# Sparse attention in a two-block transformer kernel: split products of probabilities and values replaced by plain float32 ones, and the scaling of the probabilities moved into the transposing product

## The chip, the cores and the metric

The kernel runs on one core of one Trainium2 chip. The metric is the device time of one execution in microseconds. A core has a matrix engine (TensorE, PE in the profile, with its weight loads as PEld), a vector engine (VectorE, DVE), a scalar engine (ScalarE, ACT), GpSimd (POOL) and SyncE (SP). Each works through its own instructions in order, and semaphores join them. Transfers are issued from SP's and POOL's queues.

## The reference, cut to what matters

The program is two transformer blocks on 512 tokens of width 1024. The part that the change touches is the sparse attention (`nsa_mixer`) of the second block: 16 heads of width 64 in 4 groups, which share keys and values within a group. Each head attends in three branches, to compressed keys, to selected blocks and to a window, and the branches are summed with gates:

```python
p_c = masked_softmax(s_c, (cmp_end[None, :] <= t[:, None])[None, None, :, None, :])
o_c = jnp.einsum('bgqhn,bngd->bqghd', p_c.astype(v_cmp.dtype), v_cmp)
...
p_s = masked_softmax(s_s, (dist_s >= 0)[:, :, :, None, :])
o_s = jnp.einsum('bgqhk,bgqkd->bqghd', p_s.astype(v_g.dtype), v_g)
...
p_w = masked_softmax(s_w, m_w[None, None, :, None, :])
o_w = jnp.einsum('bgqhk,bkgd->bqghd', p_w.astype(vw_b.dtype), vw_b)
out = gb[..., 0:1] * o_c + gb[..., 1:2] * o_s + gb[..., 2:3] * o_w
```

Everything is float32. At 512 tokens the selected blocks and the window take in every earlier token, so that these two branches are causal attention over 512 keys, with different keys and values and the same relative bias.

## The kernel before

A matrix product of two float32 matrices is written as products of float32r halves nearly everywhere: a number is split into a high part (a copy cast to float32r on ACT) and a low part (the difference, a subtraction on DVE), and the products of the parts are summed in PSUM. `split` (L157) and `wsplit` (L212) do this, and `gemm_g` (L229) issues three products for each pair of 128x128 weights and 128x512 activations (L243 to L245).

The sparse attention runs in the phase `pa2` (L1475). Three streams are woven into one program order there by `weave` (L57), with the weights written beside them: `nsa` (the attention), `rwkv_backs` followed by `merge` (the recurrence of the other mixer, then the branch products), and `merge_gates` (a plain matrix product). The framework's scheduler makes each engine's order from this.

`nsa` goes through 4 groups, `nsa_group` (L1166) through the group's 4 heads. `nsa_pre` (L1112) prepares a group: the stacked queries, the split keys of the first of the two branches, and the compressed branch's probabilities, transposed and split into `pc`. Each head calls `attend` twice (L1192, `br` 1 and 2) with a gate, 32 calls in all. The pooling block in front calls it eight times without a gate.

`attend` (L299) works on 512 queries by 512 keys under the causal mask, in four tiles of queries of 128, 256, 384 and 512 keys. For each tile it makes the scores (L311, L312), adds the bias and takes the minimum on DVE (L313), and takes the exponential on ACT with the row's sum (L315). Then come the reciprocals and the gate (L316, L318), and each tile is scaled by them, two on ACT (L321) and two on DVE (L323). Ten blocks of 128x128 are transposed (L328) into PSUM, in four strips of 512, 384, 256 and 128 columns. Each strip is split (L330 on ACT, L331 on DVE), and two products (L332, L333) add it to the head's output `o`. Their stationary operand is V with its high part in 64 columns and its low part in the other 64, so `o` has the two parts' sums in its two halves. The compressed branch adds its share in the same way (L1188). `o_evac` (L335) sums the halves with a copy on ACT (L340) and an addition on DVE (L341).

`nsa_values` (L1155) loads a pair of groups' values and splits them (L1161 to L1164). Transfers of this stage that `self.side` issues are on POOL's queue: queries, keys, values and each head's bias tile (L1183).

Of the kernel before, what the change touches and what calls it, by code (L numbers as in the profile page):

```python
# [8 lines left out]
F32 = mybir.dt.float32  # L9
F32R = mybir.dt.float32r  # L10
I32 = mybir.dt.int32
AF = mybir.ActivationFunctionType
OP = mybir.AluOpType
# [25 lines left out]
class Gen:  # L39
# [259 lines left out]
    def attend(self, qst, kst, bias, V, o, first, last, gate=None):  # L299

        nc = self.nc
        kh, kl = kst
        st = self.f("sm", shape=(128, 32))
        m, s, r = st[:, 0:4], st[:, 4:8], st[:, 8:12]
        Pt = self.f("p", shape=(128, 1280))
        P = [Pt[:, 64 * i * (i + 1):64 * (i + 1) * (i + 2)] for i in range(4)]
        for i, pt in enumerate(P):
            w = 128 * (i + 1)
            ps = self.ps("a")
            qt = qst[:, i * 128:i * 128 + 128]  # L310
            nc.tensor.matmul(ps[:, :w], qt, kh[:, :w], start=True, stop=False)  # L311
            nc.tensor.matmul(ps[:, :w], qt, kl[:, :w], start=False, stop=True)  # L312
            nc.vector.tensor_tensor_reduce(pt, ps[:, :w], bias[:, 512 - w:], 1.0, 3e38, OP.add, OP.min,  # L313
                                           m[:, i:i + 1])
            nc.scalar.activation(pt, pt, AF.Exp, bias=m[:, i:i + 1], scale=-1.0, accum_out=s[:, i:i + 1])  # L315
        nc.vector.reciprocal(r, s)  # L316
        if gate is not None:
            nc.vector.tensor_tensor(r, r, gate, OP.mult)  # L318
        for i, pt in enumerate(P):
            if i >= 2:  # L320
                nc.scalar.activation(pt, pt, AF.Copy, scale=r[:, i:i + 1])  # L321
            else:
                nc.vector.tensor_scalar(pt, pt, r[:, i:i + 1], None, op0=OP.mult)  # L323
        for j in range(4):
            w = 512 - 128 * j
            ps = self.ps("b")
            for i in range(j, 4):
                nc.tensor.transpose(ps[:, (i - j) * 128:(i - j + 1) * 128], P[i][:, j * 128:j * 128 + 128], self.ident)  # L328
            ph, pl = self.f("pt", F32R), self.f("pt", F32R)
            nc.scalar.copy(ph[:, :w], ps[:, :w])  # L330
            nc.vector.tensor_tensor(pl[:, :w], ps[:, :w], ph[:, :w].bitcast(F32), OP.subtract)  # L331
            nc.tensor.matmul(o[:, j * 128:], V(j), ph[:, :w], start=first and j == 0, stop=False)  # L332
            nc.tensor.matmul(o[:, j * 128:], V(j), pl[:, :w], start=False, stop=last and j == 3)  # L333
# [724 lines left out]
    def nsa_compressed(self):  # L1058
        nc, A, V, S = self.nc, self.A, self.nc.vector, self.nc.scalar
        k = lambda n, w: self.rp.tile([128, w], F32R, name=n, tag=n, bufs=1)  # L1060
        self.cmp = kc2, vc = (k("kch", 128), k("kcl", 128)), k("vc", 512).rearrange("p (g s d) -> p g s d", g=4, s=2)
        self.gt = self.rp.tile([128, 4, 48], F32, name="gt", tag="gt", bufs=1)
        self.nsa_consts()
        yield 3.0
        w2 = self.const("w2kv", [128, 2, 192])
        nc.sync.dma_start(w2, A["c2"].rearrange("k p n -> p k n"))

        def load(i):
            t = self.f("src")
            nc.sync.dma_start(t, self.kvd[i])  # L1070
            return t
        hk = yield from self.compress([load(0), load(1)], "k")
        yield 10.0
        p = self.ps("b")
        for ct in range(2):
            nc.tensor.matmul(p[:, :128], w2[:, ct, 0:128], hk[ct], start=ct == 0, stop=ct == 1)
        kc, sq = self.f("f")[:, :128], self.f("f")[:, :128]
        S.copy(kc, p[:, :128])
        S.activation(sq, kc, AF.Square)
        col = self.norm_col(sq[:64])  # L1080
        p = self.ps("b")
        nc.tensor.transpose(p[:, :128], col[:, 0:1].to_broadcast([128, 128]), self.ident)
        V.scalar_tensor_tensor(kc, kc, self.vec("k_gain", 0), p[:, :128], OP.mult, OP.mult)
        kch, kcl = kc2
        S.copy(kch, kc)
        V.tensor_tensor(kcl, kc, kch.bitcast(F32), OP.subtract)
        hv = yield from self.compress([load(2), load(3)], "v")
        yield 10.0
        p = self.ps("b")[:, :256].rearrange("p (g d) -> p g d", g=4)
        hx = []  # L1090
        for ct in range(2):
            hx.append(self.f("f"))
            S.copy(hx[ct].rearrange("p (g h n) -> p g h n", g=4, h=4),
                   hv[ct].rearrange("p (g n) -> p g n", g=4)[:, :, None].to_broadcast([128, 4, 4, 32]))
        for g in range(4):
            for ct in range(2):
                nc.tensor.matmul(p[:, g], hx[ct][:, 128 * g:128 * g + 128], w2[:, ct, 128:192], start=ct == 0, stop=ct == 1)
        S.copy(vc[:, :, 0], p)
        V.tensor_tensor(vc[:, :, 1], p, vc[:, :, 0].bitcast(F32), OP.subtract)
        yield 1.0  # L1100

    def norm_col(self, sq):
# [9 lines left out]
    def nsa_pre(self, g):  # L1112
# [4 lines left out]
        kst = {1: self.split(k1, tag="kst")}  # L1117
# [30 lines left out]
        ps = self.ps("b")  # L1148
        for i in range(4):
            nc.tensor.transpose(ps[:, i * 128:i * 128 + 128], e[:, i * 128:i * 128 + 128], self.ident)  # L1150
        pc = self.split(ps, tag="pc")
        yield 2.0
        return qst, kst, pc

    def nsa_values(self, gp):  # L1155
        nc, V, S = self.nc, self.nc.vector, self.nc.scalar
        VT = self.VT = self.f("vt", F32R, (128, 4 * 4 * 128)).rearrange("p (t k n) -> p t k n", t=4, k=4)
        for t2 in range(2):
            z = self.f("ld").rearrange("p (t k d) -> p t k d", t=2, d=64)
            for t in range(2):  # L1160
                self.side.dma_start(z[:, t].rearrange("p k d -> p (k d)"), self.vd[gp, 2 * t2 + t])  # L1161
            v = VT[:, 2 * t2:2 * t2 + 2]
            S.copy(v[:, :, :, 0:64], z)
            V.tensor_tensor(v[:, :, :, 64:128], z, v[:, :, :, 0:64].bitcast(F32), OP.subtract)  # L1164

    def nsa_group(self, g, qst, kst, pc):  # L1166

# [7 lines left out]
        for h in range(4):  # L1175
            hd = 4 * g + h
            par = h % 2
            if par == 0:
                O = self.f("o")
            if h == 2 and g < 3:  # L1180
                self.ahead = self.nsa_loads(g + 1)
            bias = self.f("bias")
            self.side.dma_start(bias, bass.AP(tensor=self.grd.tensor, offset=self.grd.offset + hd * 1280 + 127,  # L1183
                                              ap=[[576, 2], [-1, 64], [1, 512]]))
            o = self.ps("o")
            hs = slice(32 * h, 32 * h + 32)
            for i in range(2):
                nc.tensor.matmul(o, vc[hs, g].rearrange("p s d -> p (s d)"), pc[i][hs], start=i == 0, stop=False)  # L1188
            ready = self.nsa_pre(g + 1) if h == 3 and g < 3 else iter(())
            for br in (1, 2):  # L1190
                kv = 2 * (br - 1) + gl
                self.attend(qst[h], kst[br], bias, lambda j: VT[:, j, kv], o,  # L1192
                            False, br == 2, gate=self.gt[:, :, 3 * hd + br])
                yield 3.6
                if br == 1:
                    try:
                        while True:
                            yield next(ready)
                    except StopIteration as done:
                        pre = done.value  # L1200
            self.o_evac(O, o, par)
            if par == 1:
                pr = hd // 2
                nc.sync.dma_start(self.ynd[pr], O)
                if "y_n" in self.dbg:
                    nc.sync.dma_start(self.dbg["y_n"][pr * 128:(pr + 1) * 128], O)
# [30 lines left out]
    def merge(self, live):  # L1237
# [29 lines left out]
            yield w  # L1267
        while "" in live:
            yield None
        load, product_n = self.branch(A["w_br_n"], self.ynd, 8, second, ["kst"] * 3 + ["qst"] * 2 + ["pt"] * 2 + [("p", 1280)],  # L1270
                                      "f", "f")
        yield from self.side_by_side([product, load])
        yield from self.side_by_side([product_n, residual()])
# [169 lines left out]
def emit(tc, A, out, dbg={}):  # L1443
    nc = tc.nc
    with ExitStack() as ctx:
# [14 lines left out]
        with g.phase("rec"):  # L1460
# [11 lines left out]
                g.weave(("", g.rwkv_fronts(xs), 245), ("_p", others(), 170))  # L1472
            g.banks = {"a": "01", "b": "23", "n": "2", "o": "4", "a_b": "5", "b_b": "6", "g_m": "7", "g_b": "56"}
            g.side = nc.gpsimd
            with g.phase("pa2", f=3, ld=3, qst=5, kst=6, p=2, pt=4, bias=2, pc=2, kz=1, o=1, ot=1, vt=1,  # L1475
                         kb=1, v=1, bk=1, ys=1, vs=2, vu=2, yc=6, vgb=2, y=2, f_m=1, **{"as": 1}):
                g.reserve(kb=1024, v=512, vs=1024, vu=1024, yc=128, bk=1024, y=1024, ys=1024,
                          vgb=512, ld=512, kst=512, vt=2048, qst=512, f=512, pc=512, bias=512)

                live = {"", "_m"}  # L1480

# [146 lines left out]
```

## Time and profile before

| what | value |
|---|---|
| median of 3 runs | 2083.45 us (2080.49 to 2084.88) |
| the profiled execution | 2082.19 us, span of its instructions 2080.4 us |
| mean granted TensorE clock over the span | 0.981 |
| PE, PEld busy | 2004.5 us (96%), 1627.0 us (78%) |
| DVE, ACT, POOL busy | 1308.6 us (63%), 925.3 us (44%), 95.5 us (5%) |

Busy time is the union of an engine's records. Records of matmuls are pipelined: one begins before the one ahead of it has ended, so their lengths don't add up to time, and their distances do. L12 is line 12 of the kernel. `x32` counts instructions. "out<-in" names the tiles.

### The profile page before, as it was taken

What the parts mean: (1) busy time and instruction counts of PE and PEld (TensorE: products, weight loads), DVE (VectorE), ACT (ScalarE), POOL (GpSimd) and SP (SyncE); (2) the same over time, 40 slices, a digit from 0 to 9 for tenths busy, and PEclk for the clock granted to TensorE, in tenths of its full rate; (3) what the DMA queues carried; (4) which work ended last, traced back from release to release, by engine and by line L of the source; (5) the groups of instructions that cost most, each with busy time, mean ns of one, the idle gap of its engine ahead of it and who ended that gap; (6) DMA issues with size and microseconds to landing.
All of it is one profiled execution on the core that took longest, in us unless ns stands there. A gap on an engine that the chain in (4) does not pass through costs nothing.

```text
span 2080.4 us, 27852 instructions
## 1 busy us (share of the span) xinstructions
PE 2004.5 (96%) x9927; PEld 1627.0 (78%) x9927; DVE 1308.6 (63%) x3007; ACT 925.3 (44%) x1778; POOL 95.5 (5%) x167
## 2 busy tenths in 40 slices
PE   8999999999999899899988899999999999999999
PEld 7778888888888677777767687887878778888887
DVE  5785432554463568687848988888466756666522
ACT  4874531442254233333346577777243443333311
POOL 0000000000003200000120111000000000000000
PEclk9999999999999999999989899999999999999999
DMA  5222332333355754755673445446442123333332
GB/s 161 82 85 93 99 93 92 117 108 120 117 185 158 171 147 141 183 147 168 191 168 105 129 122 145 126 123 190 154 140 84 41 81 92 101 92 98 95 109 84
DMA packets 178267, 256.75 MB, mean 123 GB/s; under 512 B 95409, under 2 KB 109953, under 8 KB 178129
## 3 DMA queue, kind: packets, MB, share of 16 engines
q1 hardware_dynamic: 162832, 231.31, 38.2%
q0 software_dynamic: 15296, 23.66, 3.9%
q8 instruction: 79, 1.29, 0.3%
q14 instruction: 60, 0.48, 0.1%
HBM read 205.12 MB, written 45.53 MB: 120 GB/s over the span
## 4 chain that ended last, share of the span: by engine, by line
PE 46%; DVE 6%; ACT 3%; issue 2%; DMA 2%; SPq 0%; POOL 0%; DVEq 0%; ACTq 0%; POOLq 0%
PE psg L243 8%; PE psg L245 8%; PE psg L244 8%; PE psg_b L243 1%; PE psg_b L244 1%; PE psg_b L245 1%; PE psb L328 1%; DVE ys L777 1%; PE psg_p L243 1%; PE psg_p L244 1%; PE psg_p L245 1%; PE pso L332 1%; PE psa L744 1%; DVE ys L778 1%; PE pso L333 1%
## 5 line engine op out<-in xcount | busy, mean ns | idle before, releaser
L222 ACT CAST wh<-ws 128x1024 fp32r<-128x1024 f32 (+2 forms) x283 | 291.6, 1031 | 697.9 <-PE psg L244 457.1
L223 DVE TENSOR_TENSOR wl<-ws,wh 128x1024 fp32r<-128x1024 f32 (+2 forms) x283 | 339.4, 1201 | 266.3 <-ACT wh L222 265.7
L243 PE MATMUL psg<-xh,wh 128*128 128x512 f32 x984 | 392.2, 399 | 4.7 <-ACT wh L222 4.7
L245 PE MATMUL psg<-xh,wl 128*128 128x512 f32 x984 | 393.1, 399 | 0.0
L244 PE MATMUL psg<-act,wh 128*128 128x512 f32 x912 | 359.7, 395 | 1.1 <-DVE act L166 1.1
L243 PEld LDWEIGHTS psg<-xh,wh 128*128 128x128 f32 x984 | 186.0, 189 | 46.8 <-ACT wh L222 5.5
L245 PEld LDWEIGHTS psg<-xh,wl 128*128 128x128 f32 x984 | 186.0, 189 | 41.5 <-issue 1.2
L244 PEld LDWEIGHTS psg<-act,wh 128*128 128x128 f32 x912 | 171.1, 188 | 42.8 <-DVE act L166 1.5
L243 PE MATMUL psg<-act,wh 128*128 128x512 f32 x496 | 196.1, 397 | 2.8 <-ACT act L165 1.4
L245 PE MATMUL psg<-act,wl 128*128 128x512 f32 x496 | 196.1, 396 | 0.5 <-DVE wl L223 0.5
L244 PE MATMUL psg<-xl,wh 128*128 128x512 f32 x352 | 139.7, 397 | 0.0
L243 PEld LDWEIGHTS psg<-act,wh 128*128 128x128 f32 x496 | 92.8, 188 | 27.2 <-ACT act L165 2.2
L245 PEld LDWEIGHTS psg<-act,wl 128*128 128x128 f32 x496 | 93.0, 187 | 23.7 <-DVE wl L223 1.3
L315 ACT ACTIVATE p<-p,sm 128x128 f32<-128x128 f32 (+3 forms) x160 | 89.6, 561 | 15.0 <-DVE sm L313 13.6
L331 DVE TENSOR_TENSOR pt<-psb,pt 128x512 fp32r<-128x512 f32 (+3 forms) x160 | 75.8, 487 | 20.0 <-ACT pt L330 17.7
L244 PE MATMUL psg<-x,wh 128*128 128x512 f32 x216 | 88.2, 409 | 0.0
L313 DVE CUSTOM_DVE_ANT_0 p<-psa,bias 128x128 f32<-128x128 f32 (+3 forms) x160 | 75.9, 485 | 8.2 <-PE psa L312 6.1
L328 PE MATMUL psb<-ident,p 128*128 128x128 f32 x400 | 75.3, 285 | 2.5 <-DVE y L921 0.9
L244 PEld LDWEIGHTS psg<-xl,wh 128*128 128x128 f32 x352 | 66.3, 188 | 14.0
L330 ACT CAST pt<-psb 128x512 fp32r<-128x512 f32 (+3 forms) x160 | 65.8, 424 | 25.7 <-PE psb L328 20.8
L243 PE MATMUL psg_p<-xh,wh 128*128 128x512 f32 x176 | 73.3, 416 | 1.1 <-ACT f L957 0.6
L244 PE MATMUL psg_p<-x,wh 128*128 128x512 f32 x176 | 72.2, 410 | 0.0
(491 smaller groups left out, 3899.1 us busy)
## 6 DMA issues: line engine op xcount, KB each, us to landing
ws<-in_w_in SPq DMA_DIRECT2D x49, 512.0 KB, 4.0
ws<-in_w_fup SPq DMA_DIRECT2D x44, 512.0 KB, 3.5
ws<-in_w_up SPq DMA_DIRECT2D x32, 512.0 KB, 3.5
ws<-in_w_down SPq DMA_DIRECT2D x32, 512.0 KB, 3.6
ws<-in_w_fdn SPq DMA_DIRECT2D x16, 512.0 KB, 3.6
ws<-in_w_qku SPq DMA_DIRECT2D x12, 512.0 KB, 3.6
ws<-in_w_in POOLq DMA_DIRECT2D x10, 512.0 KB, 4.6
ws<-in_w_out SPq DMA_DIRECT2D x8, 512.0 KB, 3.5
```

Source lines behind the costliest of these rows:

```text
L222: nc.scalar.copy(wh[:, :n], ws[:, :n])
L223: nc.vector.tensor_tensor(wl[:, :n], ws[:, :n], wh[:, :n].bitcast(F32), OP.subtract)
L243: nc.tensor.matmul(p[:, :n], wh[:, s], h[:, :n], start=c + k == 0, stop=False)
L244: nc.tensor.matmul(p[:, :n], wh[:, s], l[:, :n], start=False, stop=False)
L245: nc.tensor.matmul(p[:, :n], wl[:, s], h[:, :n], start=False, stop=last)
L313: nc.vector.tensor_tensor_reduce(pt, ps[:, :w], bias[:, 512 - w:], 1.0, 3e38, OP.add, OP.min, m[:, i:i + 1])
L315: nc.scalar.activation(pt, pt, AF.Exp, bias=m[:, i:i + 1], scale=-1.0, accum_out=s[:, i:i + 1])
L328: nc.tensor.transpose(ps[:, (i - j) * 128:(i - j + 1) * 128], P[i][:, j * 128:j * 128 + 128], self.ident)
L330: nc.scalar.copy(ph[:, :w], ps[:, :w])
L331: nc.vector.tensor_tensor(pl[:, :w], ps[:, :w], ph[:, :w].bitcast(F32), OP.subtract)
L332: nc.tensor.matmul(o[:, j * 128:], V(j), ph[:, :w], start=first and j == 0, stop=False)
L333: nc.tensor.matmul(o[:, j * 128:], V(j), pl[:, :w], start=False, stop=last and j == 3)
```

## The change

In the gated calls of `attend` the tiles are no longer scaled. The vector engine writes four diagonal matrices of the reciprocals (`dg`) in one instruction, and each block's transpose becomes a plain matrix product of the block with its diagonal, which transposes and scales at once. Each strip is copied from PSUM as float32, and one plain float32 product with the unsplit V (64 columns) adds it to the upper half of `o`. The compressed branch's probabilities and values are not split either. `o` is copied by ACT without the addition. V is loaded straight into its tile. Buffers change with it: `kst` 6 to 4, `dg` 2, `pc` 2 to 1, `o` 1 to 2, `ot` gone, `vt` half as wide. The ungated calls stay as they are.

```diff
@@ attend
-        for i, pt in enumerate(P):
-            if i >= 2:
-                nc.scalar.activation(pt, pt, AF.Copy, scale=r[:, i:i + 1])
-            else:
-                nc.vector.tensor_scalar(pt, pt, r[:, i:i + 1], None, op0=OP.mult)
+        if gate is not None:
+            dg = self.f("dg").rearrange("p (i n) -> p i n", i=4)
+            nc.vector.tensor_tensor(dg, self.ident[:, None, :].to_broadcast([128, 4, 128]),
+                                    r[:, :, None].to_broadcast([128, 4, 128]), OP.mult)
+        else:
+            dg = None
+            for i, pt in enumerate(P):
+                if i >= 2:
+                    nc.scalar.activation(pt, pt, AF.Copy, scale=r[:, i:i + 1])
+                else:
+                    nc.vector.tensor_scalar(pt, pt, r[:, i:i + 1], None, op0=OP.mult)
         for j in range(4):
             w = 512 - 128 * j
             ps = self.ps("b")
             for i in range(j, 4):
-                nc.tensor.transpose(ps[:, (i - j) * 128:(i - j + 1) * 128], P[i][:, j * 128:j * 128 + 128], self.ident)
+                src, dst = P[i][:, j * 128:j * 128 + 128], ps[:, (i - j) * 128:(i - j + 1) * 128]
+                if dg is not None:
+                    nc.tensor.matmul(dst, src, dg[:, i], start=True, stop=True)
+                else:
+                    nc.tensor.transpose(dst, src, self.ident)
+            if gate is not None:
+                pf = self.f("pt")
+                nc.scalar.copy(pf[:, :w], ps[:, :w])
+                nc.tensor.matmul(o[:64, j * 128:], V(j), pf[:, :w], start=first and j == 0, stop=last and j == 3)
+                continue
             ph, pl = self.f("pt", F32R), self.f("pt", F32R)
@@ nsa_compressed
-        self.cmp = kc2, vc = (k("kch", 128), k("kcl", 128)), k("vc", 512).rearrange("p (g s d) -> p g s d", g=4, s=2)
+        self.cmp = kc2, vc = (k("kch", 128), k("kcl", 128)), k("vc", 256).bitcast(F32).rearrange("p (g d) -> p g d", g=4)
...
-        S.copy(vc[:, :, 0], p)
-        V.tensor_tensor(vc[:, :, 1], p, vc[:, :, 0].bitcast(F32), OP.subtract)
+        S.copy(vc, p)
@@ nsa_pre
-        pc = self.split(ps, tag="pc")
+        pc = self.f("pc")
+        S.copy(pc, ps)
@@ nsa_values
-        VT = self.VT = self.f("vt", F32R, (128, 4 * 4 * 128)).rearrange("p (t k n) -> p t k n", t=4, k=4)
-        for t2 in range(2):
-            z = self.f("ld").rearrange("p (t k d) -> p t k d", t=2, d=64)
-            for t in range(2):
-                self.side.dma_start(z[:, t].rearrange("p k d -> p (k d)"), self.vd[gp, 2 * t2 + t])
-            v = VT[:, 2 * t2:2 * t2 + 2]
-            S.copy(v[:, :, :, 0:64], z)
-            V.tensor_tensor(v[:, :, :, 64:128], z, v[:, :, :, 0:64].bitcast(F32), OP.subtract)
+        VT = self.VT = self.f("vt", shape=(128, 4 * 4 * 64)).rearrange("p (t k d) -> p t k d", t=4, k=4)
+        for t in range(4):
+            self.side.dma_start(VT[:, t].rearrange("p k d -> p (k d)"), self.vd[gp, t])
@@ nsa_group
-            for i in range(2):
-                nc.tensor.matmul(o, vc[hs, g].rearrange("p s d -> p (s d)"), pc[i][hs], start=i == 0, stop=False)
+            nc.tensor.matmul(o[:64], vc[hs, g], pc[hs], start=True, stop=False)
...
-            self.o_evac(O, o, par)
+            nc.scalar.copy(O[64 * par:64 * par + 64], o[:64])
@@ merge: buffers for the second branch's operands
-["kst"] * 3 + ["qst"] * 2 + ["pt"] * 2 + [("p", 1280)]
+["kst"] * 2 + ["dg"] + ["qst"] * 2 + ["pt"] * 2 + [("p", 1280)]
@@ emit, phase pa2
-f=3, ld=3, qst=5, kst=6, p=2, pt=4, bias=2, pc=2, kz=1, o=1, ot=1, vt=1
+f=3, ld=3, qst=5, kst=4, dg=2, p=2, pt=4, bias=2, pc=1, kz=1, o=2, vt=1
```

## Rows read from the trace of the kernel before

**Rows 1.** The page: busy time, share of the span and instructions of each engine.
```profile
PE 2004.5 (96%) x9927; PEld 1627.0 (78%) x9927; DVE 1308.6 (63%) x3007; ACT 925.3 (44%) x1778; POOL 95.5 (5%) x167
```

**Rows 2.** Stretches: length, busy (instructions) by engine, PE clock, DMA share, GB/s.
```profile
1055.00:1200.00 145.00, 123.59 (x666) 100.81 (x666) 116.58 (x381) 88.80 (x250) 19.40 (x32) 0.87 0.54 135
1200.00:1450.00 250.00, 241.29 (x1484) 197.57 (x1484) 211.45 (x715) 192.88 (x535) 18.81 (x29) 0.99 0.50 139
1800.00:1900.00 100.00, 100.00 (x434) 81.19 (x433) 64.42 (x82) 36.85 (x45) 0.00 (x0) 1.00 0.30 95
```

**Rows 3.** Timeline of PE, three places: start us, us, line, tiles, shapes, count.
```profile
1141.72 0.92 PE L328 MATMUL psb<-ident,p 128*128 128x128 f32 x7
...
1204.33 0.28 PE L333 MATMUL pso<-pt,vt 128*128 128x256 f32 x1
1204.45 0.27 PE L332 MATMUL pso<-pt,vt 128*128 128x128 f32 x1
1204.56 0.45 PE L244 MATMUL psg_m<-x,wh 128*128 128x512 f32 x1
...
1208.39 0.34 PE L332 MATMUL pso<-pt,vt 128*128 128x384 f32 x1
1208.57 0.36 PE L333 MATMUL pso<-pt,vt 128*128 128x384 f32 x1
```

**Rows 4.** Groups of PE by line and shape, 1200:1450: busy, mean ns | idle before.
```profile
L328 PE MATMUL psb<-ident,p 128*128 128x128 f32 x233 | 43.4, 279 | 1.7 <-DVE y L921 0.9 <-ACT p L321 0.7
L244 PE MATMUL psg_m<-x,wh 128*128 128x512 f32 x55 | 23.7, 431 | 0.0
...
L1188 PE MATMUL pso<-pc,vc 32*128 32x512 f32 x22 | 8.5, 453 | 0.1
...
L245 PE MATMUL psg_b<-as,wl 128*128 128x512 f32 x1 | 0.4, 392 | 0.0
```

**Rows 5.** Timeline of PE at two plain float32 products, 114 and 691 us.
```profile
114.56 1.02 PE L485 MATMUL psn<-sq,wp 128*128 128x512 f32 x2
115.01 0.62 PE L332 MATMUL pso<-pt,VT 128*128 128x128 f32 x1
...
690.82 0.72 PE L744 MATMUL psa<-ar,kb 64*128 64x128 f32 x5
```

**Rows 6.** Single lines: ns min/median/max, first and last start, forms.
```profile
L485 PE MATMUL psn<-sq,wp x8: 591/592/643, 114.6 to 148.1; 128*128 128x512 f32 x8
L874 PE MATMUL psb_b<-vs,ws x128: 270/275/582, 1067.9 to 1408.2; 128*128 128x128 f32 x128
L973 PE MATMUL psb<-f,tab x10: 188/587/597, 682.2 to 698.7; 32*16 32x512 f32 x6, 32*16 32x32 f32 x2, 32*16 32x128 f32 x2
```

**Rows 7.** Groups of DVE and ACT over the span, shapes together: busy, mean ns.
```profile
L331 DVE TENSOR_TENSOR pt<-psb,pt 128x512 fp32r<-128x512 f32 (+3 forms) x160 | 75.8, 487 | 20.0 <-ACT pt L330 17.7
L321 ACT ACTIVATE p<-p,sm 128x384 f32<-128x384 f32 x80 | 50.1, 662 | 4.4 <-DVE sm L318 3.4 <-DVE sm L316 0.4
L323 DVE TENSOR_SCALAR p<-p,sm 128x128 f32<-128x128 f32 x80 | 22.4, 316 | 0.4
L341 DVE TENSOR_TENSOR o<-pso,ot 64x512 f32<-64x512 f32 x24 | 16.5, 686 | 2.5 <-ACT ot L340 2.1
L1147 DVE TENSOR_TENSOR f<-f,sm 128x512 f32<-128x512 f32 x4 | 2.7, 684 | 0.0
```

**Rows 8.** Waits of PEld, 1200:1450: us in total, times, longest.
```profile
PEld pso L332 <- ACT pt L330: 10.6, 34, 0.8
PEld pso L333 <- DVE pt L331: 4.8, 13, 1.7
PEld psb L328 <- ACT p L321: 1.6, 5, 0.6
```

**Rows 9.** The chain of waits, 1055:1100: start us, us, what.
```profile
1070.35 13.11 DMA kb<-kbd
```

**Rows 10.** Landing of the value transfers, L1161.
```profile
DMA to landing us min/median/max: 3.6/7.1/7.9
```

More of the change, by code (lines that the diff above doesn't have):

```diff
@@ L1155, in nsa_values @@
     def nsa_values(self, gp):
-        nc, V, S = self.nc, self.nc.vector, self.nc.scalar
-        VT = self.VT = self.f("vt", F32R, (128, 4 * 4 * 128)).rearrange("p (t k n) -> p t k n", t=4, k=4)
-        for t2 in range(2):
-            z = self.f("ld").rearrange("p (t k d) -> p t k d", t=2, d=64)
-            for t in range(2):
-                self.side.dma_start(z[:, t].rearrange("p k d -> p (k d)"), self.vd[gp, 2 * t2 + t])
-            v = VT[:, 2 * t2:2 * t2 + 2]
-            S.copy(v[:, :, :, 0:64], z)
-            V.tensor_tensor(v[:, :, :, 64:128], z, v[:, :, :, 0:64].bitcast(F32), OP.subtract)
+        VT = self.VT = self.f("vt", shape=(128, 4 * 4 * 64)).rearrange("p (t k d) -> p t k d", t=4, k=4)
+        for t in range(4):
+            self.side.dma_start(VT[:, t].rearrange("p k d -> p (k d)"), self.vd[gp, t])
     def nsa_group(self, g, qst, kst, pc):
@@ L1269, in merge @@
             yield None
-        load, product_n = self.branch(A["w_br_n"], self.ynd, 8, second, ["kst"] * 3 + ["qst"] * 2 + ["pt"] * 2 + [("p", 1280)],
+        load, product_n = self.branch(A["w_br_n"], self.ynd, 8, second, ["kst"] * 2 + ["dg"] + ["qst"] * 2 + ["pt"] * 2 + [("p", 1280)],
                                       "f", "f")
@@ L1474, in emit @@
             g.side = nc.gpsimd
-            with g.phase("pa2", f=3, ld=3, qst=5, kst=6, p=2, pt=4, bias=2, pc=2, kz=1, o=1, ot=1, vt=1,
+            with g.phase("pa2", f=3, ld=3, qst=5, kst=4, dg=2, p=2, pt=4, bias=2, pc=1, kz=1, o=2, vt=1,
                          kb=1, v=1, bk=1, ys=1, vs=2, vu=2, yc=6, vgb=2, y=2, f_m=1, **{"as": 1}):
                 g.reserve(kb=1024, v=512, vs=1024, vu=1024, yc=128, bk=1024, y=1024, ys=1024,
-                          vgb=512, ld=512, kst=512, vt=2048, qst=512, f=512, pc=512, bias=512)
+                          vgb=512, ld=512, kst=512, vt=1024, qst=512, f=512, pc=512, bias=512)
                 live = {"", "_m"}
```

## The prediction, made before the changed kernel was run

> **What bounds the kernel now.** I read the page first: the matmul engine (PE) is busy for 96% of the span, with the weight loads beside it [rows 1]. That figure is a union of records that last longer than the distance at which they start, so it doesn't say how much room PE has. The table of stretches comes next [rows 2]. The change lies where the gated calls of `attend` run, 1055 to 1450 us. In the pure matrix products of 1800:1900, 434 products of 512 columns fill 100 us, 0.23 us each: PE has no room there. In 1200:1450 the vector engine (DVE) is busy 85%, ACT 77%, and PE starts 1,484 products in 250 us.
>
> How full PE really is there follows from the distance between starts [rows 3]: 0.23 us for 512 columns, 0.18 for 384, 0.12 for 256, 0.11 for 128 (seven transposes take 0.92, the last of them 0.27, so 0.108 each). In the list of products of 1200:1450 [rows 4], 339 records in 30 groups are 512 wide (the first and the last of these groups are shown), 92 are 384 wide, 92 are 256 wide and 961 are 128 or less. So 339 x 0.23 + 92 x 0.18 + 92 x 0.12 + 961 x 0.11 = 211 us of 250: PE is 84% full and stands 39 us. At the same 0.142 us a record, the 666 records of 1055:1200 are 95 us of 145: 65% full. DVE is 80% busy there, and the chain of waits shows a transfer of 13 us at its beginning [rows 9].
>
> The reader is to see two regimes: up to 1200 DVE and arrivals set the pace and PE has room; from 1200 on PE, DVE and ACT are all nearly full. After 1450 there are matrix products again, so what is late in this stage is late at the end.
>
> **The change part by part.** Of the 400 transposes 80 belong to the eight ungated calls, which stay; 320, ten in each of 32 calls, are changed. By the 233 records of rows 4, 23.3 calls lie in 1200:1450 and 8.7 before.
>
> *A plain float32 product on PE.* The trace before holds such products, though not these. The code's 64 products at L874 are 128 records, and L485's four are eight: each is two passes [rows 6]. At 512 columns two passes take 1.02 us and one alone 0.59, so the second starts 0.43 after the first, and the narrow product behind it, which lasts 0.62, is held up [rows 5]. At 128 columns five passes take 0.72 with a last one of 0.27: 0.112 each [rows 5, 6]. For 384 and 256 columns I scale 0.43: 0.32 and 0.215. Could the narrower stationary operand (64 columns for 128) make it cheaper? L973, with 32 rows and 16 columns, lasts 0.59 like L485's 128 by 128 [rows 6], so I take no discount.
>
> *Values.* Before, two products for each of the four widths: 2 x (0.23 + 0.18 + 0.12 + 0.11) = 1.28 us a call. After, one product of two passes: 2 x (0.43 + 0.32 + 0.215 + 0.11) = 2.15. Added: 0.87.
>
> *Normalising transposes.* Before 10 x 0.108 = 1.08, after 10 x 2 x 0.112 = 2.24. Added: 1.16. The Trainium skill ("TensorE: Matmul & The Clock Gate", Terms) speaks against this part: the transpose mode, which these ten give up, makes float32 four times faster, so by it the ten would come to 4.3 us. The trace agrees only in the sign: one transpose takes hardly less than one pass, and a product is two.
>
> *Compressed branch.* The 32 records at L1188 stay 32, as two passes instead of two products: 0.43 for 0.23, 6.4 us in all.
>
> PE together: 32 x (0.87 + 1.16) + 6.4 = 71 us more, of which 23.3 x 2.03 + 22 x 0.2 = 52 in 1200:1450 and 20 before.
>
> *DVE.* A call loses four subtractions (L331, mean 0.487) and two scalings (L323, 0.316) and gains the diagonal, a 128x512 product with a broadcast operand like L1147, 0.684: 1.95 + 0.63 - 0.68 = 1.90 [rows 7]. Times 32 that is 61; 16 sums of L341 (0.686) are 11; eight subtractions of the size of L1147 (four `pc`, four V) are 5.5. Together 77 us less, 21 of them before 1200 by the share of calls. *ACT* loses 2 x 0.662 a call (L321), 42 us; the copies of L330 stay.
>
> *Waits.* The second value product waited for the subtraction: the weight load of L333 stood 4.8 us for it. That goes. L332 stood 10.6 for the copy, and L328 1.6 for the scaling [rows 8]; both should shrink with ACT and DVE lighter, since the diagonal (0.68) stands where two ACT scalings (1.32) stood.
>
> *Buffers.* V now arrives straight in its one buffer, so the four transfers of groups 2 and 3 wait on POOL's queue until the last value product of group 1, with the next bias loads behind them; they take 7.1 us to land [rows 10]. That delays one stream once, while the recurrence and the gate products keep PE supplied: 0, or up to 7 without that cover. `kst` goes from six buffers to four: new keys wait for the last score product of the old ones, with one call in between; 0, or one copy and one subtraction, 1.4, for each of seven key pairs.
>
> **Sum.** *1200:1450.* PE's work becomes 211 + 52 = 263, more than the stretch. To it comes what PE still stands. Of the 39 us, 17 are the three waits above; I leave 6 of these and 16 of the other 22, because a fuller queue hides some: 22. That makes 285, or +35. *1055:1200.* PE's 95 + 20 still fit into 145. DVE loses 21 of its 117; if it alone set the pace all 21 would be saved, and if arrivals did, none. I take 12, a little over half, since only the first thirty us are marked by transfers. Net +23. The profiled execution took 2082.2 us (span 2080.4 and 1.8 around it; the median of the runs is 1.3 higher): 2082 + 23 = 2105.
>
> **The rivals.**
> *DVE is the pacer and PE swallows it.* Mechanism: with 77 us less on DVE, PE is fed without a break. For it: DVE is 85% busy and its subtraction delays L333. Against: 263 us don't go into 250. At the 98% fill that only pure products reach [rows 2] the stretch takes 268, +18; with all 21 saved before 1200 the sum is -3, and if the first stretch saves more than 21 it ends at 2065 to 2079. It decides when PE stands no more than some 5 us in the second stretch. Chance 14%.
> *They cancel.* PE stands about 10 us and the first stretch saves its 21: 2079 to 2086. Chance 8%.
> *PE's work is only added.* PE's waits belong to the recurrence (L874, L888, L891 and the vector work between), and stay 39; then 1200:1450 alone is +52, and with nothing saved before, 2134; with the 20 us of the first stretch added as well, 2153. Chance 10%.
> *The transposing product costs four transposes, not 2.1.* Then 320 x 3 x 0.108 = 104 us are added in place of 37, which gives 2105 + 67 = 2172. Against it: passes of 128 columns would have to start 0.22 apart, and L744's start 0.112 apart. Chance 2%. The rule of the page named above leads here.
>
> **How the numbers follow.** The forecast, PE full from 1200 on and a part given back before, has 66%, for 2087 to 2134. The 8-in-10 range adds the case in which they cancel and the upper part of the faster one, 2075 to 2134. About 0.2%, 4 us, is what a measurement of this kernel tells from no change. Slower by more: 66 + 10 + 2 = 78%. Within: 8%. Faster: 14%.
>
> **What would show it.** In place of L328, two records a product, 0.112 apart; the value product as two records, 0.43 apart at 512 columns; 320 PE records more in all; DVE's busy time down by about 77 us and ACT's by about 42; DVE's busy share in the second stretch near 65% with PE's starts closing up; L333's wait gone; the stage ending near 1473. Wrong would be the forecast if the stage still ends by 1450, if passes on a 64-column operand start closer than 0.4 us, or if PE stands as long as before although DVE is free.

## The result, and the profile after

The changed kernel takes 2134.3 us (median of 4 runs, 2130.1 to 2142.5) against 2082.0 for the one before: 1.0256 times as long, with a 95% interval of 1.0227 to 1.0285. That is 52 us slower by the medians (53 by the ratio), where 23 were forecast, and just above the forecast's range, which ended at 2134. The direction and the engine were right, the size was not.

The page of the changed kernel, the row of busy time and instructions, which answers to [rows 1]; then its stretches, which answer to [rows 2]:

```profile
PE 2065.2 (97%) x10247; PEld 1638.7 (77%) x10247; DVE 1250.4 (59%) x2822; ACT 890.2 (42%) x1710; POOL 95.1 (4%) x167
```
```profile
1055.00:1200.00 145.00, 128.89 (x740) 96.25 (x739) 97.67 (x327) 72.67 (x220) 13.37 (x21) 0.94 0.49 118
1200.00:1450.00 250.00, 246.52 (x1472) 183.69 (x1472) 142.28 (x519) 140.08 (x415) 16.73 (x26) 1.00 0.42 113
1450.00:1495.00 45.00, 41.73 (x188) 24.71 (x186) 22.14 (x53) 25.48 (x63) 0.00 (x0) 0.92 0.46 149
```

There are exactly 320 PE records more, one for each transpose that became two passes. DVE loses 58 us and ACT 35. In 1200:1450 DVE's share fell from 85% to 57% and ACT's from 77% to 56%, and still the stage's last value product starts at 1494.8, where it started at 1448.6 before (the last transposes at 1493.5 and 1447.2). So neither of them sets the pace there any more. The chain of waits in 1200:1450, by line, names PE at the head; before, L328 had 7.2% of it and L332 and L333 together 11.2%:

```profile
by line: PE pso L342 17.1%; PE psb L336 15.5%; PE psa_b L894 4.3%; PE psb_b L903 4.3%; PE psb_b L906 4.1%; PE psb_b L889 4.0%; PE pso L1196 3.6%; PE psa L311 3.5%; PE psg_m L243 3.3%; PE psa L312 3.3%; PE psg_m L245 3.2%; PE psa_b L896 3.1%
```

The two new products as single lines, which answer to [rows 6] (L336 transposes with the diagonal, L342 multiplies by the values), the second with its weight loads:

```profile
L336 PE MATMUL psb<-dg,p x640: 270/275/582, 1074.1 to 1493.5; 128*128 128x128 f32 x160
...
L342 PEld LDWEIGHTS pso<-pt,vt x256: 132/136/231, 1076.1 to 1494.6; 128*64 128x64 f32 x128
L342 PE MATMUL pso<-pt,vt x256: 272/486/1114, 1076.1 to 1494.8; 128*64 128x512 f32 x32, 128*64 128x384 f32 x32, 128*64 128x256 f32 x32, 128*64 128x128 f32 x32
```

What the sum did not hold is seen in the timeline of PE, three neighbouring rows of the changed kernel, with the weight load of the third below (a row that joins several passes gives the shape of its first):

```profile
1308.61 0.61 PE L336 MATMUL psb<-dg,p 128*128 128x128 f32 x4
1309.15 1.72 PE L342 MATMUL pso<-pt,vt 128*64 128x512 f32 x4
1310.80 0.94 PE L336 MATMUL psb<-dg,p 128*128 128x128 f32 x6
```
```profile
1310.80 0.74 PEld L336 LDWEIGHTS psb<-dg,p 128*128 128x128 f32 x6 [0.60 <-issue]
```

The first group ends at 1309.22 and the four value passes at 1310.87, 1.65 later. Two passes of 512 columns and two of 384 are 2 x 0.43 + 2 x 0.32 = 1.50. The next six passes end 0.87 after them, and are 6 x 0.112 = 0.67. So 0.15 us are lost where the stationary operand goes from 128 columns to 64, and 0.20 where it goes back. At the way back the profile shows nothing that was waited for: the weight load of the third group began only at 1310.80, after standing 0.60 us with no releaser ("issue"), together with its product and not ahead of it. The Trainium skill ("TensorE: Matmul & The Clock Gate", Part 2) says that PE's queue pulls the next weight load ahead of running products. The trace agrees inside the groups, where each load of the third group's later passes starts a product ahead, and not at the change of width. In the trace the width changes 90 times each way (going in, 74 times at L342 and 16 at L1196): 90 x 0.35 = 32 us, an estimate from this one place.

### The profile page after: what moved, and what is told of

The parts are those of the page before. It is cut to its first block, busy times and chain, and to the rows that moved or that the text cites. A ratio compares the mean times of both kernels' runs of the same rounds, so it can differ in the third digit from the quotient of the medians.

```text
span 2130.9 us, 28263 instructions
## 1 busy us (share of the span) xinstructions
PE 2065.2 (97%) x10247; PEld 1638.7 (77%) x10247; DVE 1250.4 (59%) x2822; ACT 890.2 (42%) x1710; POOL 95.1 (4%) x167
## 4 chain that ended last, share of the span: by engine, by line
PE 51%; DVE 4%; DMA 2%; ACT 2%; issue 1%; SPq 0%; DVEq 0%; ACTq 0%
PE psg L244 8%; PE psg L243 8%; PE psg L245 8%; PE pso L342 4%; PE psb L336 3%; PE psg_b L245 1%; PE psg_b L243 1%; PE psg_b L244 1%; PE psg_p L243 1%; DMA vu<-vs 1%; PE psg_p L244 1%; PE psg_p L245 1%; DVE ys L792 1%; PE psa L311 1%; PE pso L1196 1%
## 5 line engine op out<-in xcount | busy, mean ns | idle before, releaser
L336 PEld LDWEIGHTS psb<-dg,p 128*128 128x128 f32 x640 | 81.1, 195 | 32.8 <-issue 23.3
L336 PE MATMUL psb<-dg,p 128*128 128x128 f32 x640 | 94.2, 288 | 4.1 <-DVE dg L321 4.0
L341 ACT COPY pt<-psb 128x512 f32<-128x512 f32 (+3 forms) x128 | 51.1, 426 | 90.9 <-PE psb L336 89.6
L342 PE MATMUL pso<-pt,vt 128*64 128x512 f32 (+3 forms) x256 | 87.0, 455 | 1.1 <-ACT pt L341 1.1
```

The lines of the kernel that those rows point to most:

```text
L336: nc.tensor.matmul(dst, src, dg[:, i], start=True, stop=True)
L341: nc.scalar.copy(pf[:, :w], ps[:, :w])
L342: nc.tensor.matmul(o[:64, j * 128:], V(j), pf[:, :w], start=first and j == 0, stop=last and j == 3)
```

## The experiments

Ratios are to the kernel before, run beside each version on the same chip. Its median there lay between 2081.0 and 2085.0 us, so ratios are compared here and not medians; a difference of two ratios is uncertain by some 0.002 to 0.004 (4 to 9 us).

| run | what it is | us (median) | ratio, 95% interval |
|---|---|---|---|
| wide | the change, 128 stationary columns | 2118.1 | 1.0168 (1.0137 to 1.0199) |
| diag | diagonal only | 2107.7 | 1.0127 (1.0096 to 1.0157) |
| values_wide | values only, 128 columns | 2084.6 | 1.0015 (0.9997 to 1.0033) |
| strip1 | before, last strip plain | 2078.9 | 0.9981 (0.9963 to 1.0) |
| values | values only, 64 columns | 2096.2 | 1.0071 (1.0047 to 1.0094) |
| wide_rows | wide, 128 rows in the compressed branch | 2116.9 | 1.0155 (1.0134 to 1.0177) |
| values_wide_rows | values_wide, likewise | 2084.7 | 0.9998 (0.9981 to 1.0015) |
| strip2 | before, last two strips plain | 2083.2 | 0.9991 (0.9978 to 1.0005) |
| wide_p3 | wide, three probability buffers | 2111.2 | 1.0161 (1.0143 to 1.0179) |
| values_wide_p3 | values_wide, likewise | 2080.5 | 0.9996 (0.998 to 1.0012) |
| plain_t | before, plain products with the identity | 2099.9 | 1.0077 (1.0057 to 1.0096) |
| strip1_all | strip1 in the ungated calls too | 2076.7 | 0.9972 (0.9958 to 0.9986) |
| kst4 | before, four key buffers | 2084.7 | 1.0017 (1.0004 to 1.003) |
| diag_parts | diag, the diagonal in four instructions | 2108.3 | 1.0119 (1.0104 to 1.0134) |
| values_wide_k6 | values_wide, six key buffers | 2086.9 | 1.0021 (1.0006 to 1.0036) |

**The width: wide and values.** The value products and the compressed branch's products take 128 columns. The second 64 are whatever lies next in the tile, other V columns or zeros at its end, and go into the half of `o` that nobody reads (cut; the compressed product at L1200 and the slightly longer tiles are left out here):

```diff
-self.attend(qst[h], kst[br], bias, lambda j: VT[:, j, kv], o,
+self.attend(qst[h], kst[br], bias, lambda j: VT[:, 256 * j + 64 * kv:256 * j + 64 * kv + 128], o,
-                nc.tensor.matmul(o[:64, j * 128:], V(j), pf[:, :w], start=first and j == 0, stop=last and j == 3)
+                nc.tensor.matmul(o[:, j * 128:], V(j), pf[:, :w], start=first and j == 0, stop=last and j == 3)
```

> The changed kernel with its plain value products and its compressed-branch products on a stationary operand of 128 columns instead of 64 (the next 64 columns of the same tile are taken along, and the lower half of the output tile is not used); passes, moving columns and every other engine's work stay. Theory A (a change of the stationary operand's width holds up PE): in the trace of the changed kernel the first pass on 64 columns comes 0.14 us late and the first 128-column pass behind it 0.19 us late, some 91 times, 31 us in all; without it the time falls by 25 to 31 us, to 2103 to 2109, and the idle time of PE in the stage falls by as much. Theory B (PE's idle time belongs to the recurrence and to the waits for copies): the time stays within 4 us of 2134.

It took 2118.1: the ratio falls by 0.0088, 18 us with an uncertainty of some 9. The direction is theory A's, the size two thirds of what it said. The same sequence of passes at another place in this run's timeline:

```profile
1129.06 0.61 PE L336 MATMUL psb<-dg,p 128*128 128x128 f32 x4
1129.50 1.70 PE L342 MATMUL pso<-pt,vt 128*128 128x512 f32 x4
1131.04 0.83 PE L336 MATMUL psb<-dg,p 128*128 128x128 f32 x6
```

From the start of the first to the end of the last it is 2.81 us, where the narrow operand took 3.13. The waits of PE's weight loads in 1200:1450, first of the changed kernel, then of this one:

```profile
PEld psb L336 <- issue: 11.2, 19, 0.8
PEld pso L342 <- ACT pt L341: 8.2, 25, 0.8
```
```profile
PEld pso L342 <- ACT pt L341: 7.1, 21, 0.8
...
PEld psb L336 <- issue: 3.1, 10, 0.5
```

L336's waits without a releaser go from 11.2 to 3.1 us, while the loads of the value products wait for the strip's copy nearly as long as before (8.2 and 7.1). The trace also shows why 32 us were not gained: only the way out of the value products is mended. Over the whole stage, the first 128-column passes behind a value product came 0.20 us late in the changed kernel (the median of 74 places) and 0.00 in "wide" (71); the first passes of a value product came 0.15 late (72) and still 0.12 (71). In sum the ways out fell from 16.5 to 0.8 us and the ways in from 13.1 to 11.6, together 17 us, which fits the 18 measured. (These are estimates: distances between the starts of PE's records in 1050:1500, less the prices above, where the granted clock was at its upper level.)

The second pair differs in the width alone as well. This run has the values part as the change has it, without the diagonal:

```diff
-        if gate is not None:
+        if False:
             dg = self.f("dg").rearrange("p (i n) -> p i n", i=4)
```

> The values part alone as the change has it, on 64 columns: scalings and transposes as before, plain value products. It differs from the run on 128 columns (2084.6) in the width alone. Theory A (each change of the stationary operand's shape holds PE up): slower than that run by about what the width was worth in the whole change, 16 us: 2096 to 2105. Theory B (the width mattered only because PE was overfull with the diagonal's products): within 5 us of 2085, as PE has slack here.

2096.2, at the lower edge of what theory A said: the ratio is 0.0056 above that on 128 columns, 12 us with an uncertainty of some 6, also without the diagonal's passes on PE. Counted as above, the ways out of the value products are 0.15 us late here (the median of 70) and 0.00 on 128 columns. The operand's width and the height of the output in PSUM change together in both pairs, so the two aren't told apart.

**The two parts: diag and values_wide.**

```diff
# diag: dg and the products with it as in the change; scalings dropped; the split value products stay
+                nc.tensor.matmul(dst, src, dg[:, i], start=True, stop=True)
# values_wide: the edit of "wide", with "if False" at dg
# both with the change's buffers, kst=4 and dg=2 (cut)
```

> Only the diagonal part of the change: gated calls transpose and normalise by the plain product with the diagonal, and the values are multiplied as before by two split products on 128 columns. PE gets 320 x 0.116 = 37 us more, ACT loses 42 us, DVE stays. If PE's work decides: 2105 to 2119 (37 us, less what a lighter ACT gives back). If DVE sets the pace of the stage, whose work doesn't change: within 5 us of 2082. There is no 64-column operand, so neither late start of theory A may be seen at it.

> Only the other part, on 128 columns: scaling on ACT and DVE and transposes as before; plain float32 value products and compressed-branch products on a 128-column stationary operand. PE gets 28 + 6 = 34 us more, DVE loses some 79 us, ACT stays as before but for the V casts. If PE's work decides and its idle time stays: 2116. If the lighter DVE closes PE's idle time, since 211 + 25 us of work still fit into the 250 us of the second stretch: 2075 to 2095.

The diagonal costs 26 us (1.0127) for 37 us more of PE's work, within what that work foretold. The values on 128 columns cost 3 us (1.0015, an interval that takes in no change) for 34 us more. In the stretch 1200:1450 of the two runs (columns as in [rows 2]):

```profile
1200.00:1450.00 250.00, 239.79 (x1545) 205.88 (x1544) 192.48 (x636) 148.14 (x435) 17.77 (x28) 0.97 0.45 124
```
```profile
1200.00:1450.00 250.00, 240.71 (x1365) 182.88 (x1366) 153.95 (x572) 176.83 (x494) 16.33 (x26) 0.99 0.47 130
```

The diagonal leaves DVE at 77% and empties ACT, to 59%; the values empty DVE, to 62%, and leave ACT at 71%. Nearly all of PE's extra passes come back with the values and less than a third of them with the diagonal. The wait for the strip's copy isn't what shrank: in 1200:1450 the load of L342 stood 18.3 us for it in "values_wide", where L332 stood 10.6 before [rows 8].

**The size of an operand's rows: wide_rows and values_wide_rows.** The compressed branch's stationary operand has 32 rows, and the records show late starts there too:

```diff
+        for h in range(4):
+            hs = slice(32 * h, 32 * h + 32)
+            nc.scalar.copy(self.vz[hs, h], vc[hs, 64 * g:64 * g + 128])
-            nc.tensor.matmul(o, vc[hs, 64 * g:64 * g + 128], pc[hs], start=True, stop=False)
+            nc.tensor.matmul(o, self.vz[:, h], pc, start=True, stop=False)
```

> The changed kernel on 128 columns, and its compressed-branch products on all 128 rows as well: for each head a stationary operand that is zero outside that head's 32 rows, four small copies on ACT a group. Theory A says that a change of the rows holds PE up as one of the columns does: in the trace the first 32-row pass comes 0.42 us late and the 128-row pass behind it 0.22, 16 times each, 10 us. Then 5 to 10 us less than 2118: 2108 to 2113. If only the column count matters, 2118 within 3.

> The same edit of the compressed branch on the values part alone (2084.6 without it). By theory A the late starts at 32 rows are 16 x 0.21 and 16 x 0.18, 6 us, of which a half or more is gained: 2078 to 2082. If rows don't matter: 2085 within 3.

The ratios fall by 0.0013 and 0.0017, 3 us, less than their intervals. In the trace the late starts do go: counted as above, the compressed product came 0.20 us late in "wide" and 0.05 in "wide_rows", and the pass behind it 0.19 and 0.00 (medians of 15 or 16 places each). Whether that is worth anything in the time is not shown.

**Plain strips in the kernel before: strip1, strip2, strip1_all.** The split V serves as one float32 operand of 128 columns, and `o_evac` adds the halves as ever:

```diff
+            if gate is not None and j >= 3:       # strip2: j >= 2; strip1_all: without the gate
+                pf = self.f("pt")
+                nc.scalar.copy(pf[:, :w], ps[:, :w])
+                nc.tensor.matmul(o[:, j * 128:], V(j).bitcast(F32), pf[:, :w], start=False, stop=last and j == 3)
+                continue
```

> The kernel before with one edit: the last strip of each gated call (128 columns) is not split, but copied as float32 and multiplied by one plain float32 product with the split V as its 128-column stationary operand. Two passes of 0.11 us stand for two products of 0.11 us, so PE has the same work; DVE loses 32 subtractions of 0.286 us, 9 us. If DVE sets the pace of the stage: 2073 to 2079. If PE does: within 2 us of 2082.

> The kernel before with the last two strips of a gated call (256 and 128 columns) as plain float32 products on the split V. DVE loses 32 x (0.42 + 0.29) = 23 us; PE gets 32 x (0.43 - 0.24) = 6 us more. If what DVE loses comes back at the rate of the values part (79 us of DVE and 34 us of PE made +3, so some 0.4 us for each us of DVE): 2081 + 6 - 9 = 2078. If PE's work decides: 2087.

> The last strip as a plain product, in the gated calls (0.9981 of the kernel before, with an interval up to 1.0) and in the eight ungated ones too. PE's work is the same as before; DVE loses 40 x 0.286 = 11 us. If DVE's pace counts: 0.996 to 0.999. If the gated run's gain was chance: 1.000 within 0.001.

strip1 gives 0.9981 with an interval that just reaches 1, strip2 nothing that can be told from no change, strip1_all 0.9972 (0.9958 to 0.9986), 6 us less than the kernel before: the one version here whose interval lies wholly below 1. Its plain product as a single line:

```profile
L332 PE MATMUL pso<-pt,vt x64: 270/275/421, 1082.9 to 1440.9; 128*128 128x128 f32 x64
```

Two passes of 128 columns stand for two split products of 128 columns, and one subtraction on DVE is gone.

**Calls in flight: wide_p3 and values_wide_p3.** `p=2` becomes `p=3` in the phase.

> The changed kernel on 128 columns (2118) with three probability buffers instead of two, so that three calls can be under way at once. PE still stands some 71 us between 1040 us and the end of the branch products there, though DVE is only 57% busy. Theory C (this is the latency of a call's chain, with too few calls under way): PE's idle time falls and the time with it, to 2100 to 2112. Theory D (PE's order and the recurrence's chain set it): within 4 us of 2118.

> The values part on 128 columns (1.0015 of the kernel before) with three probability buffers. Theory C: 2070 to 2080, 0.993 to 0.999 of the kernel before, which would beat both kernels. Theory D: 0.2% either way of 1.0015.

1.0161 for 1.0168 and 0.9996 for 1.0015: nothing clear of the intervals. The medians, 2111.2 and 2080.5, lie at the edge of what theory C said, and by the ratios a gain of up to some 9 us is not excluded. Theory C is not borne out, but it isn't refuted either; why PE still stands stays open.

**What the diagonal costs: plain_t, kst4, diag_parts, values_wide_k6.**

```diff
# plain_t, in gated calls
-                nc.tensor.transpose(dst, src, self.ident)
+                nc.tensor.matmul(dst, src, self.ident, start=True, stop=True)
# kst4
-qst=5, kst=6,
+qst=5, kst=4, dg=2,
# diag_parts
-            nc.vector.tensor_tensor(dg, self.ident[:, None, :].to_broadcast([128, 4, 128]), r[:, :, None]..., OP.mult)
+            for i in range(4):
+                if i >= 2:
+                    nc.scalar.activation(dg[:, i], self.ident, AF.Copy, scale=r[:, i:i + 1])
+                else:
+                    nc.vector.tensor_scalar(dg[:, i], self.ident, r[:, i:i + 1], None, op0=OP.mult)
# values_wide_k6
-qst=5, kst=4, dg=2,
+qst=5, kst=6,
```

> The kernel before with one edit: in the gated calls the ten transposes are plain float32 products with the identity, so two passes of 0.112 us instead of one of 0.108; the scalings on ACT and DVE stay, and there is no diagonal. PE gets the same 37 us as in the run with the diagonal alone (1.0127), and nothing is taken from ACT. If that run's cost is PE's work and the 42 us of ACT gave something back, this one is slower than it: 1.014 to 1.019. If ACT's relief is worth nothing: 1.0127 within 0.002.

The expectation missed. With every scaling still in place, the same 37 us on PE cost 16 us (1.0077), less than with the diagonal (26). So more than half of the added passes came back with no engine relieved, and taking 42 us from ACT while waiting for the diagonal made a net loss of some 10 us more (3 to 18 by the intervals). What ACT's relief alone is worth was not measured. Two explanations of the 10 us were tried:

> The kernel before with the change's buffers alone: four key tiles instead of six, and the two diagonal tiles allocated, which only the branch products use later. No engine's work changes. Theory E (the key buffers make up the difference between the diagonal, 1.0127, and plain transposes alone, 1.0077): 1.003 to 1.006. Theory F (the diagonal makes it: all ten products of a call wait for one DVE instruction behind the last tile): 1.000 within 0.0015.

> The diagonal part alone (1.0127) with the four diagonal matrices written by four instructions, two on DVE and two on ACT, as the scalings were, so that the first strip's first product waits for 128 columns and not for 512. Four key tiles as there. Theory F: 1.006 to 1.010, near plain transposes alone. Theory E: 1.0127 within 0.002.

> The values part on 128 columns (1.0015) with six key tiles and no diagonal tiles. Theory E: it gains what four tiles cost, 0.996 to 0.999, and beats the kernel before. Theory F: 1.0015 within 0.002.

The buffers alone cost 0.0017, 3.5 us, about half of what theory E asked, and from the other side (values_wide_k6) their return gives nothing. Four small instructions for one large move nothing (1.0119 for 1.0127): theory F falls, and the trace of "diag" agrees, where the loads of L336 stood only 1.0 us in all for the diagonal. So of the 10 us at most some 3 are the buffers, and the rest, near the intervals' width, stays open.

**A rival that no run separates: the granted clock.** In 1055:1200 TensorE's mean granted clock was 0.87 before [rows 2] and 0.94 in the changed kernel; in single profiled executions it was 0.95 in "values_wide", 0.92 in "plain_t" and 0.88 in "diag". Its two levels are 1.2 and 2.4 GHz, so 0.87 means some 38 of the 145 us at the lower one, and 0.95 some 15 (estimates, twice the missing share times 145). What that level costs is seen in the changed kernel's chain of waits, at a place where the granted clock was 0.50, behind a stand of 3.77 us for the diagonal, and at one where it was 1.00:

```profile
1151.65 3.35 PE psb L336 x14
...
1356.58 1.76 PE psb L336 x14
```

Over all executions the mean clock was 0.979 for the kernel before (23 executions beside "diag" and "values_wide"), 0.987 for "values_wide", 0.984 for "plain_t" and 0.981 for "diag". Of these three, the ones that got more of PE's passes back are those with the higher clock. Whether the clock gave the time back, or only followed from a PE that stood less, is not shown; some of the 10 us between "diag" and "plain_t" may be it too.

## Why the prediction was right in direction and wrong in size

*A plain product is two passes, at 0.43 and 0.112 us.* Right: 320 records more, and the timeline above fits 0.112 for the diagonal's passes and 0.43 and 0.32 for the values'.

*"I take no discount" for the narrower operand.* This step failed. I asked only whether 64 columns could be cheaper, and took the passes' price from operands whose neighbours had the same width. Passes on 64 columns follow each other at the same distance as on 128, but the way back to 128 columns costs 0.20 us each time, and the way in 0.15, most of which (0.12) was lost on 128 columns too. It is a term of the sum that was missing, 18 us in the time (12 without the diagonal; the two agree within their uncertainty).

*"A fuller queue hides some": PE's 39 us of standing become 22.* This step failed too. The three waits did shrink in the changed kernel, from 17.0 to 9.0 us (8.2 for the copy, 0.8 for the diagonal; 6 were forecast). But by the prediction's own prices the records of 1200:1450 make 217 us of work in the changed kernel and 216 in "wide", so that PE stood 33 and 34 of the 250 us (estimates). Without the waits that is 24 and 26, where 22 were to become 16. In the changed kernel 14.6 of it are the loads of L336 and L342 that stood without a releaser.

*The stretch before 1200 gives 12 us back.* Not decided. The counts of transposes before 1200 say how far each kernel was (ten a call before, twenty after), first the kernel before, then the changed one, then "wide":

```profile
1055.00:1200.00 145.00, 17.14 (x87) 12.76 (x87) 0.87 0.54 135
...
1055.00:1200.00 145.00, 28.21 (x186) 24.22 (x186) 0.94 0.49 118
...
1055.00:1200.00 145.00, 26.58 (x200) 25.30 (x200) 0.95 0.48 123
```

That is 8.7, 9.3 and 10.0 calls. At 10.7 us a call (23.3 in 250 us) the changed kernel was some 6 us ahead at 1200 and "wide" 14. From there to the stage's end (its last transposes at 1493.5; 1474.8 in "wide", 1447.2 before) the changed kernel then lost 53 us and "wide" 42, where 35 were forecast; behind the stage it is another 4 and 2. So the sum went wrong behind 1200. These are single executions: "kst4", whose engines have the work of the kernel before, had done 9.5 calls at 1200, so the split is good to some 9 us and the gift before 1200 may be nothing. The 65% at which the prediction saw PE full there is also too low, since it used full-clock prices in a stretch whose mean granted clock was 0.87.

*Both parts are credited with the relief of DVE and ACT.* Right for neither as it stands. In "plain_t" nothing is relieved and 21 of 37 us come back; at that rate the values' 34 us would cost some 15 (an estimate), and they cost 3, so that the lighter DVE, or the clock that rose with it, is worth some 12 of DVE's 79. The diagonal's 42 us off ACT show no gain: "plain_t", which keeps them, is the faster one. Without the width the change costs 35 us (1.0168) where I had 23.

*The whole*: 3 for the values, 16 for the passes of the transposes, 10 for the diagonal and its buffers, 18 for the width, and the 6 that are left over, which no run measured by themselves: 53.

*DVE 77 us less, ACT 42 less.* Right. The page shows 58 and 35, but it counts overlapping records once. The lengths of DVE's records add up to 1454 us before and 1379 after, those of ACT's to 1009 and 964: 75 and 45 less.

*Buffers at nothing.* Nearly: kst4 costs 3.5 us. For V's single buffer nothing was tried apart, but in the changed kernel no load of L342 is shown to wait for V's transfers, and these waited once for L342, 1.8 us.

*The rivals.* That DVE is the pacer and PE swallows the change is false for the whole, and close to true for the values part. That PE's work is only added, with PE's waits unchanged, gave 52 to 71 us. Its 2134 is the measured time partly by luck, since it has no term for the width, and on 128 columns half of its 71 us came back; but from 1200 on PE stood nearly as long as before, as it said. Four transposes' price for the diagonal product is refuted by 0.112.

## What to carry to other kernels

When a matrix product's operands change shape, price the neighbours too: a product on 64 stationary columns among products on 128 can cost more than its own passes show, and filling the unused columns with whatever lies beside them took 18 of 53 us off here. An engine that is 96% busy by its records can still have room: it took in more than half of 37 us of added passes with nothing else changed. Before a cheaper vector engine is paid for with matrix passes, split the edit into parts and time each: here the part that emptied DVE came out even on 128 columns, and the part that emptied ACT lost. A plain float32 product was a gain (6 us) only on 128 moving columns, where a pass took no longer than a split product; with 256 columns as well no difference was found.

## What the runs showed of the hardware that had not been expected

Behind passes on 64 stationary columns the next weight load on 128 columns lost its place ahead of the running product: the load stood 0.60 us and started together with its product, and the products behind came 0.20 us late, the median of 74 places. On 128 columns throughout the delay was 0.00 (71 places), and the same sequence of 14 passes took 2.81 us for 3.13. The weight loads on 64 columns were themselves shorter, 136 ns for 189 in "wide" at the median, but the passes still started 0.43 us apart at 512 columns.
